# Turning the softmax weights of sixteen heads: 32 x 32 squares on VectorE and a way through DRAM in place of TensorE transposes

## The chip, the cores and the metric

The kernel runs on one core of a Trainium2 chip. The metric is the device time of one execution in microseconds (us). Before the change three runs took 2202.40, 2202.78 and 2203.02 us, a median of 2202.78 us. The engines are called by the profile's names: PE is TensorE's matmul, PEld its weight load, DVE is VectorE, ACT is ScalarE, POOL is GpSimd, SP is SyncE. A "q" behind a name (SPq, POOLq) is the queue on which that engine issues transfers.

## The reference, cut to what matters

The model is a trunk of two layers for 256 tokens of 2048 features: a gated linear attention layer, then a cross-decoder layer with 16 heads of 128 features, each followed by a gated feed-forward network with a short convolution. The change touches the second layer's attention alone. With a block of 256 and a sequence of 256 there is only the query's own block, so it is plain causal attention with a bias by distance:

```python
def attend(c):
    ...
    s_own = jnp.einsum('bhqd,bhkd->bhqk', q_c, k_own).astype(jnp.float32)
    s_own = s_own + bias_table[:, rel_bucket(dist_own)][None]
    s_own = jnp.where(dist_own >= 0, s_own, -jnp.inf)
    scores = jnp.concatenate([s_sel.reshape(B, H, QC, topk * BLK), s_own], axis=-1)
    p = jax.nn.softmax(scores, axis=-1).astype(v_blk.dtype)
    ...
    return (jnp.einsum('bhqjk,bhqjkd->bhqd', p_sel, v_sel)
            + jnp.einsum('bhqk,bhkd->bhqd', p_own, v_own))
```

Keys and queries are normed per head first. The weights p come out with queries on the rows; the product with v contracts over keys, so p is needed with keys on the rows, that is, turned.

## The kernel before, in words

**Weights.** All large matmuls read float32 weights, split into a high part (`whi`, a cast to the reduced float type that TensorE takes) and a low rest (`wlo`). `WeightStream` cuts every weight matrix into chunks of 128 x 2048 (1 MB, three `wraw` buffers, loaded on SP's queue at L112) and each chunk into halves of 1024 columns. `prefetch` makes `whi` of a half on ScalarE (L132) and `wlo` on VectorE (L133); there are four buffers of each. `step` takes the next half; all other work hangs on these steps: `after(n, job)` puts a job n steps ahead, and `step` runs the jobs that are due before it takes its half.

**The stage around the change.** `gemm_tok` (L348) works through 16 row tiles in eight steps: per step eight matmuls with `whi` (L357) and four with `wlo` (L360) into one accumulator. It runs four times for the queries, four times for the keys (weights `w_kk`) and four times for the values (`w_kv`); each run covers four heads.

- `head_norm` (L917) norms a key group. ScalarE squares and copies (L921, L922), VectorE reduces (L924, L925), GpSimd takes a power (`rr`, L927), VectorE multiplies (L929).
- `features` (L932), three and four steps later, turns the group on TensorE (`tr`, L937), ScalarE and VectorE copy and split it (L940 to L943).
- `softmax` (L949), five to eight steps after the key group, does the scores of one head on TensorE (L953 for the first 128 queries against 128 keys, L955 three times for the other 128 queries against all 256 keys), then on VectorE adds the bias and finds the extreme (L962), on ScalarE takes the exponential with its sum (L964), on VectorE the reciprocal (L966) and the scaling (L968). The result `s` is 128 queries x 384: columns 0 to 127 for the first half of the queries, 128 to 383 for the second.
- `turn` (L971), two steps after each head's softmax, makes three 128 x 128 transposes on TensorE into the PSUM tile `pT` (L975). The first 256 columns of `pT` are split into a high and a low part in `p0` (`split`: L382 on ScalarE, L383 on VectorE), the last 128 are copied to `p1` on ScalarE (L981).
- `values` (L983), one and two steps after each value group, multiplies them with v (`mix`, L429, tile `o`) and splits the result (`ox`).

**Other work in the stage.** `make_ahead` (L306) prepares sums of the second feed-forward's down weights: SP loads a 1 MB plane into one of two `ahead` buffers (L314), VectorE does four additions (L311, L312), POOL writes it to DRAM (`tsum`, L321). Later in the kernel `turn_h` (L796) turns the residual by a VectorE transpose in squares of 32 (L801) and eight transfers on SP's queue with runs of 128 B (`hscr`, L807).

**Memory.** Small PSUM tiles (`s`, `pT`, `tr`, `o` and others) share two banks. Most SBUF tiles of the stage take one of 32 slots of equal size. Temporary tiles such as `s` take one of six.

**Order.** Each engine works through its own list in order. The lists come from a planner that models the time of each instruction; `tc.issue_after(x)` keeps what is inside it behind instruction x on the same engine. `ws.low` is the latest `wlo`, `ws.load` the latest weight load. Every instruction waits for what it reads and for the buffer it writes; a transfer also waits for its turn on one of eight completion counters per kind of queue.

Of the kernel before, what the change touches and what calls it, by code (L numbers as in the profile page):

```python
# [8 lines left out]
F32 = mybir.dt.float32  # L9
# [16 lines left out]
MH = 16  # L26
# [32 lines left out]
class WeightStream:  # L59
# [58 lines left out]
    def prefetch(self, i):  # L118
        nc = self.nc
        while self.n_split < len(self.halves):  # L120
            n = self.n_split
            c, o, width, deep = self.halves[n]
            if n > i + self.AHEAD + deep:
                break
            self._dma(c + 1)
            t = self.tiles[c]
            src = t[o // 1024] if isinstance(t, list) else t[:, o:o + width]
            hi = self.parts.tile([128, 1024], F32R, name="whi")
            lo = self.parts.tile([128, 1024], F32R, name="wlo")
            for a, b in ((0, 512), (512, 1024)) if n < 2 else ((0, src.shape[1]),):  # L130
                with self.tc.issue_after(self.first) if n + a else nullcontext():
                    nc.scalar.copy(hi[:, a:b], src[:, a:b])  # L132
                self.low = nc.vector.tensor_sub(lo[:, a:b], src[:, a:b], hi[:, a:b].bitcast(F32))  # L133
            self.split[n] = (hi, lo)
            self.n_split += 1
            if self.chunks[c][-1] == n:
                del self.tiles[c]
                self._dma(c + (6 if c in self.quads else 4))
# [7 lines left out]
def trunk(ctx: ExitStack, tc: tile.TileContext, xT, cst, msk, w1p, w2a, w_k, w_qa, w_v2, w_v, w_g, w_go,  # L146
          w_up0, w_dn0, w_kk, w_kv, w_mq, w_mo, w_up1, w_dn1, rel, onehot, out):
    nc = tc.nc
    V, A, T = nc.vector, nc.scalar, nc.tensor
# [9 lines left out]
    dram = ctx.enter_context(tc.tile_pool(name="dram", bufs=1, space=DRAM))  # L159

    def slot(shape, dt, name):
        return big.tile(shape, dt, name=name, tag="slot")
# [4 lines left out]
    def bank(name, shape):  # L167
        return mis_ps.tile(list(shape), F32, name=name, tag="bank")

    ws = WeightStream(tc, raw, parts)  # L170
# [4 lines left out]
    for layer, todo in enumerate(ahead):  # L175
        t = dram.tile([len(todo), 128, 2048], F32, name=f"tsum{layer}")
# [55 lines left out]
    ident = mk[:, 0:128]  # L232
# [70 lines left out]
    def after(steps, job):  # L303
        later.append((cur[0] + steps, job))
# [43 lines left out]
    def gemm_tok(xs, groups=1):  # L348
        out_ = [acc_ps.tile([128, 2, 512], F32, name="acc") for _ in range(groups)]
        for q0 in range(0, KT, 2):  # L350
            for ps in out_:
                hi, lo = step()
                for ks in ((0,), (1,)) if cur[0] < 3 and groups > 1 else ((0, 1),):
                    tiles_ = [(q0 + k, t, k * 512) for k in ks for t in range(2)]
                    for x0 in (0, S):
                        for kt, t, c in tiles_:
                            T.matmul(ps[:, t, :], xs(kt)[:, x0 + 128 * t:x0 + 128 * t + 128], hi[:, c:c + 512],  # L357
                                     start=kt == 0 and x0 == 0, stop=False)
                    for kt, t, c in tiles_:
                        T.matmul(ps[:, t, :], xs(kt)[:, 128 * t:128 * t + 128], lo[:, c:c + 512],  # L360
                                 start=False, stop=kt == KT - 1)
        ws.prefetch(cur[0])
        return out_ if groups > 1 else out_[0]
# [4 lines left out]
    def both(ps, name):  # L368
        t = temp(name)
        A.copy(t, ps[:, :, S:])  # L370
        V.tensor_add(t, t, ps[:, :, :S])
        return t
# [8 lines left out]
    def split(dst_hi, dst_lo, src):  # L381
        A.copy(dst_hi, src)  # L382
        V.tensor_sub(dst_lo, src, dst_hi.bitcast(F32))  # L383
# [124 lines left out]
    for hd in range(GH):  # L508
        ps = gemm(xs, KT)
        rstd = nrm.rstd  # L510
        k = both(ps, "k")
        V.tensor_mul(k, k, bc(rstd))
        b = bcum[hd]
# [64 lines left out]
    for hd in range(GH):  # L578
        ps = gemm(xs, KT)
        q = both(ps, "q")  # L580
# [11 lines left out]
    for hd in range(GH):  # L592
        for c in range(2):
            ps = gemm(xs, KT)
            g = both(ps, "g")
# [321 lines left out]
    def head_norm(ps, name):  # L917
        t_, sq = slot([128, 2, 512], F32, name), slot([128, 2, 512], F32, "hsq")
        for t in range(2):
            r = n_q.col[:, t:t + 1]  # L920
            A.activation(sq[:, t, :], ps[:, t, :], AF.Square, scale=r)  # L921
            A.activation(t_[:, t, :], ps[:, t, :], AF.Copy, scale=r)  # L922
        ss = small.tile([128, 8], F32, name="ss")
        V.tensor_reduce(ss, sq.rearrange("p t (h d) -> p (t h) d", d=128), axis=AX.X, op=OP.add)  # L924
        V.tensor_scalar(ss, ss, 1.0 / 128, EPS, op0=OP.mult, op1=OP.add)  # L925
        rr = small.tile([128, 8], F32, name="rr")
        nc.gpsimd.tensor_tensor(rr, ss, mhalf, op=OP.pow)  # L927
        u = t_.rearrange("p t (h d) -> p (t h) d", d=128)
        V.tensor_mul(u, u, rr[:, :, None].to_broadcast([128, 8, 128]))  # L929
        return t_  # L930

    def features(t_, c, f, scale, c0):  # L932

        tp = bank("tr", (128, 2, S))
        for i in range(2):
            for t in range(2):
                T.transpose(tp[:, i, 128 * t:128 * t + 128],  # L937
                            t_[:, t, (2 * c + i) * 128:(2 * c + i + 1) * 128], ident)
        whole, halves_ = f[0][:, 2 * c:2 * c + 2, :], f[1][c]
        A.activation(whole, tp[:, :, :128], AF.Copy, scale=scale)  # L940
        hi, lo = halves_[:, :, 0, :], halves_[:, :, 1, :]
        A.activation(hi, tp[:, :, c0:], AF.Copy, scale=scale)
        V.scalar_tensor_tensor(lo, tp[:, :, c0:], scale, hi.bitcast(F32), op0=OP.mult, op1=OP.subtract)  # L943

    qf, kf, ox = [], [], []
    pts = [None] * MH
    p0s, p1s = [], []

    def softmax(hd):  # L949
        (q0, q1), (k0, k1) = qf[hd // 4], kf[hd // 4]  # L950
        q1, k1 = q1[hd // 2 % 2][:, hd % 2], k1[hd // 2 % 2][:, hd % 2]
        sp = bank("s", (128, 384))
        T.matmul(sp[:, 0:128], q0[:, hd % 4, :], k0[:, hd % 4, :], start=True, stop=True)  # L953
        for i, (a, b) in enumerate(((0, 0), (0, 1), (1, 0))):
            T.matmul(sp[:, 128:384], q1[:, a, :], k1[:, b, :], start=i == 0, stop=i == 2)  # L955
        s = temp("s", (128, 384))
        st = small.tile([128, 4], F32, name="st")
        bt = bias[hd // 4][:, hd % 4, :]
        for t, (c0, c1) in enumerate(((0, 128), (128, 384))):
            n = c1 - c0  # L960
            rev = bass.AP(tensor=bt.tensor, offset=bt.offset + n - 1, ap=[bt.ap[0], [-1, n]])
            V.tensor_tensor_reduce(s[:, c0:c1], sp[:, c0:c1], rev, -1.0, 3.0e38, OP.add, OP.min,  # L962
                                   st[:, t:t + 1])
            A.activation(s[:, c0:c1], s[:, c0:c1], AF.Exp, bias=st[:, t:t + 1], scale=-1.0,  # L964
                         accum_out=st[:, 2 + t:3 + t])
        V.reciprocal(st[:, 2:4], st[:, 2:4])  # L966
        for t, (c0, c1) in enumerate(((0, 128), (128, 384))):
            V.tensor_scalar(s[:, c0:c1], s[:, c0:c1], st[:, 2 + t:3 + t], None, op0=OP.mult)  # L968
        pts[hd] = s

    def turn(hd):  # L971
        s = pts[hd]
        tp = bank("pT", (128, 384))
        for c in range(3):
            T.transpose(tp[:, 128 * c:128 * c + 128], s[:, 128 * c:128 * c + 128], ident)  # L975
        if hd % 8 == 0:
            p1s.append(slot([128, 8, 128], F32, "p1"))
        if hd % 2 == 0:
            p0s.append(slot([128, 2, 2, S], F32R, "p0"))
        split(p0s[-1][:, hd % 2, 0], p0s[-1][:, hd % 2, 1], tp[:, :256])  # L980
        A.copy(p1s[-1][:, hd % 8], tp[:, 256:])  # L981

    def values(v, p):  # L983
        op = bank("o", (128, 2, S))
# [14 lines left out]
    for g in range(4):  # L999
# [5 lines left out]
        f = (q8[:, g % 2 * 4:g % 2 * 4 + 4], (q1[:, 0:2], q1[:, 2:4]))  # L1005
# [4 lines left out]
    for g in range(4):  # L1010
        ps = gemm_tok(xs)
        t_ = head_norm(ps, "k")
        if g % 2 == 0:
            k8 = slot([128, 8, 128], F32, "k0")
        f = (k8[:, g % 2 * 4:g % 2 * 4 + 4], [slot([128, 2, 2, S], F32R, f"k1{c}") for c in range(2)])
        kf.append(f)
        for c in range(2):
            after(3 + c, lambda t_=t_, c=c, f=f: features(t_, c, f, kqw, 0))
        for i in range(4):
            after(5 + i, lambda i=i, g=g: softmax(4 * g + i))  # L1020
            after(7 + i, lambda i=i, g=g: turn(4 * g + i))
    for g in range(4):
        ps = gemm_tok(xs)
        if g % 2 == 0:
            vm1 = slot([128, 2, 512], F32, "vm1")
        v = (slot([128, 2, 512], F32R, "vm0"), vm1[:, g % 2, :])
        v_out(v, ps, n_q)
        for c in range(2):
            after(1 + c, lambda v=v, p=2 * g + c: values(v, p))
# [115 lines left out]
```

## Time and profile before

| | |
|---|---|
| profiled execution | 2202.72 us, of which the span from the first to the last instruction is 2200.8 us |
| granted TensorE clock | 1.000 |
| transferred | 592.40 MB, mean 269 GB/s |
| transfers of 8 KB packets for weights on SP's queue (q1) | 514.79 MB, 66.1% of the 16 DMA engines |
| transfers on POOL's queue (q0) | 75.06 MB, 8.9% |
| packets under 512 B | 27,953 of 108,152 |
| transposes of the softmax weights (`pT`, L975) | 48, from 1241.4 to 1372.4 us |
| GpSimd busy over the span | 83.9 us |

How to read the profile's views: the page gives busy time by engine; matmuls overlap and their ends are modelled, so a busy TensorE is read from the chain of waits and not from its share. The chain lists the work that ended last, followed back from the end. A row of a timeline has the start, the duration, the engine, the line, the operation, the tiles (out <- in), and in brackets the idle time before it with what ended it. A row of the waits has: who waited, for whom, us in total, how often, the longest. Rows of transfers give the destination, the source, the queue, the count, the size of one and the median time from issue to landing.

### The profile page before, as it was taken

How to read it: one execution, taken by the hardware profiler on the slowest of the kernel's cores; microseconds unless marked ns; L12 is line 12 of the kernel's file. 1: busy time of each engine (PE TensorE's matmuls, PEld its weight loads, DVE VectorE, ACT ScalarE, POOL GpSimd, SP SyncE). 2: the span in 40 equal slices, each digit the busy share in tenths (PEclk: the TensorE clock that was granted, in tenths of full speed). 3: DMA queues.
4: the chain of work that ended last, by engine and by line, in shares of the span. 5: the costliest groups of instructions: out<-in, count | busy, mean ns of one | idle time of the engine just before them, and what ended most of it. 6: DMA issues, size and time to landing. Idle time of an engine off the chain costs nothing.

```text
span 2200.8 us, 31104 instructions
## 1 busy us (share of the span) xinstructions
PE 2194.0 (100%) x11689; PEld 1895.5 (86%) x11689; DVE 1763.6 (80%) x2547; ACT 1316.7 (60%) x1840; POOL 83.9 (4%) x134
## 2 busy tenths in 40 slices
PE   9999999999999999999999999999999999999999
PEld 7889888888888888888888888888888888888887
DVE  6676877888888887877777777678988888878887
ACT  6655654655566555666656655546655665556565
POOL 0000000000000000000001100000000000000000
PEclk9999999999999999999999999999999999999999
DMA  8675678777777776887768666677788777878895
GB/s 286 212 263 207 232 271 302 270 262 274 270 271 268 278 273 212 303 333 287 279 248 295 240 222 241 220 266 264 270 282 280 276 271 279 289 259 310 330 369 205
DMA packets 108152, 592.40 MB, mean 269 GB/s; under 512 B 27953, under 2 KB 28481, under 8 KB 45282
## 3 DMA queue, kind: packets, MB, share of 16 engines
q1 hardware_dynamic: 93170, 514.79, 66.1%
q0 software_dynamic: 14256, 75.06, 8.9%
q8 instruction: 91, 1.49, 0.3%
q10 hardware_dynamic: 576, 0.58, 0.1%
q14 instruction: 59, 0.48, 0.1%
HBM read 522.99 MB, written 67.40 MB: 268 GB/s over the span
## 4 chain that ended last, share of the span: by engine, by line
PE 99%; DMA 0%; ACT 0%; DVE 0%; SPq 0%; issue 0%
PE acc L342 40%; PE acc L344 21%; PE acc L736 14%; PE acc L357 10%; PE p L736 6%; PE acc L360 5%; PE sT L548 0%; DMA wraw<-w_v 0%; PE tr L937 0%; PE s L955 0%; PE pT L975 0%; PE z L454 0%; PE s L953 0%; PE o L434 0%; PE oT L434 0%; DMA gn<-cst 0%
## 5 line engine op out<-in xcount | busy, mean ns | idle before, releaser
L132 ACT CAST whi<-wraw 128x1024 fp32r<-128x1024 f32 (+1 forms) x786 | 799.1, 1020 | 629.1 <-PE acc L342 308.4
L133 DVE TENSOR_TENSOR wlo<-wraw,whi 128x1024 fp32r<-128x1024 f32 (+1 forms) x786 | 920.3, 1182 | 278.0 <-ACT whi L132 98.3
L342 PE MATMUL acc<-xw,whi 128*128 128x512 f32 x3328 | 795.5, 391 | 0.0
L342 PEld LDWEIGHTS acc<-xw,whi 128*128 128x128 f32 x3328 | 611.1, 188 | 117.9
L344 PEld LDWEIGHTS acc<-xw,wlo 128*128 128x128 f32 x3328 | 427.2, 191 | 16.2
L344 PE MATMUL acc<-xw,wlo 128*128 128x256 f32 x3328 | 433.4, 283 | 0.0
L736 PE MATMUL acc<-whi,hid 128*128 128x512 f32 x596 | 173.9, 390 | 0.0
L133 DVE TENSOR_TENSOR wlo<-ahead,whi 128x1024 fp32r<-128x1024 f32 x92 | 112.3, 1224 | 37.7 <-ACT whi L132 22.2
L357 PE MATMUL acc<-whi,xkv 128*128 128x512 f32 x512 | 132.7, 393 | 0.0
L357 PE MATMUL acc<-whi,xw 128*128 128x512 f32 x512 | 129.8, 393 | 1.5 <-ACT whi L132 1.5
L736 PEld LDWEIGHTS acc<-whi,hid 128*128 128x128 f32 x596 | 111.4, 188 | 22.8
L132 ACT CAST whi<-ahead 128x1024 fp32r<-128x1024 f32 x92 | 96.3, 1054 | 56.8 <-PE p L736 44.3
L736 PE MATMUL p<-whi,hid 128*128 128x512 f32 x386 | 124.7, 389 | 0.0
L357 PEld LDWEIGHTS acc<-whi,xw 128*128 128x128 f32 x512 | 95.3, 189 | 22.2 <-ACT whi L132 2.4
L357 PEld LDWEIGHTS acc<-whi,xkv 128*128 128x128 f32 x512 | 94.4, 188 | 18.3
L685 ACT ACTIVATE au<-up,cs 128x256 f32<-128x256 f32 x176 | 96.1, 593 | 7.6 <-DVE up L681 7.6
L687 DVE SCALAR_TENSOR_TENSOR au<-up,cs,au 128x255 f32<-128x255 f32 x176 | 82.9, 478 | 18.9 <-ACT au L685 18.8
L736 PE MATMUL acc<-wlo,hid 128*128 128x512 f32 x298 | 97.1, 389 | 0.0
L736 PE MATMUL acc<-whi,comb 128*128 128x512 f32 x320 | 95.6, 389 | 0.0
L736 PEld LDWEIGHTS p<-whi,hid 128*128 128x128 f32 x386 | 72.4, 188 | 15.1
L370 ACT COPY up<-acc 128x512 f32<-128x512 f32 x88 | 51.6, 586 | 47.0 <-PE acc L344 46.0
L689 DVE SCALAR_TENSOR_TENSOR au<-up,cs,au 128x254 f32<-128x254 f32 x176 | 79.5, 476 | 0.0
(264 smaller groups left out, 2184.7 us busy)
## 6 DMA issues: line engine op xcount, KB each, us to landing
wraw<-w_up SPq DMA_DIRECT2D x176, 1024.0 KB, 5.1
ahead<-w_dn SPq DMA_DIRECT2D x53, 1024.0 KB, 9.1
tsum<-ahead POOLq DMA_DIRECT2D x53, 1024.0 KB, 7.8
ahead<-tsum SPq DMA_DIRECT2D x46, 1024.0 KB, 6.0
wraw<-w_dn SPq DMA_DIRECT2D x53, 768.0 KB, 5.7
wraw<-w_dn SPq DMA_DIRECT2D x35, 1024.0 KB, 6.1
wraw<-w_g SPq DMA_DIRECT2D x16, 1024.0 KB, 5.7
wraw<-w_go SPq DMA_DIRECT2D x16, 1024.0 KB, 5.9
```

What stands on the lines that cost most here:

```text
L132: nc.scalar.copy(hi[:, a:b], src[:, a:b])
L133: self.low = nc.vector.tensor_sub(lo[:, a:b], src[:, a:b], hi[:, a:b].bitcast(F32))
L342: T.matmul(ps[:, b, :], two[i][0][:, c:c + 128], xs(kt), start=kt == 0, stop=False)
L344: T.matmul(ps[:, b, :S], two[i][1][:, c:c + 128], xs(kt)[:, :S], start=False, stop=kt == kts - 1)
L357: T.matmul(ps[:, t, :], xs(kt)[:, x0 + 128 * t:x0 + 128 * t + 128], hi[:, c:c + 512], start=kt == 0 and x0 == 0, stop=False)
L360: T.matmul(ps[:, t, :], xs(kt)[:, 128 * t:128 * t + 128], lo[:, c:c + 512], start=False, stop=kt == KT - 1)
L370: A.copy(t, ps[:, :, S:])
L685: A.activation(au[:, i, :], t[:, i, :], AF.Identity, bias=col(cb + n), scale=col(cw + 2 * 2 * FT + n))
L687: V.scalar_tensor_tensor(au[:, i, 1:], t[:, i, :S - 1], col(cw + 2 * FT + n), au[:, i, 1:], op0=OP.mult, op1=OP.add)
L689: V.scalar_tensor_tensor(au[:, i, 2:], t[:, i, :S - 2], col(cw + n), au[:, i, 2:], op0=OP.mult, op1=OP.add)
L736: T.matmul(p[n], x[xi], w[wi][:, 512 * f:512 * f + 512], start=n not in begun, stop=left[n] == 0)
```

## The change

`turn` no longer uses TensorE. It takes a slot tile `t` of two times 384 columns, lets VectorE transpose `s` in squares of 32 x 32 into the first half (L977 of the changed kernel), writes each quarter of 32 partitions to a DRAM tile `turned` with runs of 32 values (L980, four transfers on GpSimd's queue), and reads the head back with keys on the partitions into the second half (L981, one transfer on the same queue). The VectorE transpose is kept behind the latest `wlo`. The split into `p0` and the copy to `p1` move to a new job `weights`, eight steps after `turn`, kept behind the latest `whi` cast on ScalarE.

```diff
             for a, b in ((0, 512), (512, 1024)) if n < 2 else ((0, src.shape[1]),):
                 with self.tc.issue_after(self.first) if n + a else nullcontext():
-                    nc.scalar.copy(hi[:, a:b], src[:, a:b])
+                    self.high = nc.scalar.copy(hi[:, a:b], src[:, a:b])
                 self.low = nc.vector.tensor_sub(lo[:, a:b], src[:, a:b], hi[:, a:b].bitcast(F32))
...
+    turned = dram.tile([MH, 12, 32, 128], F32, name="turned")
+
     def turn(hd):
-        s = pts[hd]
-        tp = bank("pT", (128, 384))
-        for c in range(3):
-            T.transpose(tp[:, 128 * c:128 * c + 128], s[:, 128 * c:128 * c + 128], ident)
+
+        t = slot([128, 2, 384], F32, "pT")
+        with tc.issue_after(ws.low.ins):
+            V.transpose(t[:, 0], pts[hd])
+        to = turned[hd].rearrange("f b (m a) -> m b f a", a=32)
+        for m in range(4):
+            nc.gpsimd.dma_start(to[m], t[32 * m:32 * m + 32, 0].rearrange("b (f a) -> b f a", a=32))
+        nc.gpsimd.dma_start(t[:, 1].rearrange("k (j q) -> k j q", j=3),
+                            turned[hd].rearrange("(j f) b q -> (f b) j q", f=4))
+        pts[hd] = t[:, 1]
+
+    def weights(hd):
+        tp = pts[hd]
         if hd % 8 == 0:
             p1s.append(slot([128, 8, 128], F32, "p1"))
         if hd % 2 == 0:
             p0s.append(slot([128, 2, 2, S], F32R, "p0"))
-        split(p0s[-1][:, hd % 2, 0], p0s[-1][:, hd % 2, 1], tp[:, :256])
-        A.copy(p1s[-1][:, hd % 8], tp[:, 256:])
+        with tc.issue_after(ws.high.ins):
+            split(p0s[-1][:, hd % 2, 0], p0s[-1][:, hd % 2, 1], tp[:, :256])
+            A.copy(p1s[-1][:, hd % 8], tp[:, 256:])
...
             after(5 + i, lambda i=i, g=g: softmax(4 * g + i))
             after(7 + i, lambda i=i, g=g: turn(4 * g + i))
+            after(15 + i, lambda i=i, g=g: weights(4 * g + i))
```

## The prediction

> **What bounds the kernel now.** I read the page first: span, busy shares, and the chain of work that ended last.
>
> ```profile
> span 2200.8 us, 31104 instructions
> PE 2194.0 (100%) x11689; PEld 1895.5 (86%) x11689; DVE 1763.6 (80%) x2547; ACT 1316.7 (60%) x1840; POOL 83.9 (4%) x134
> ...
> PE 99%; DMA 0%; ACT 0%; DVE 0%; SPq 0%; issue 0%
> ```
>
> TensorE is never without work, and 99% of the chain is its own. But shares are averages, so the stage of the change comes next: the same chain in order of time, from 1200 to 1420 us.
>
> ```profile
> by line: PE acc L357 51.3%; PE acc L360 25.7%; PE acc L342 6.8%; PE acc L344 3.5%; PE s L955 2.6%; PE pT L975 2.4%; PE tr L937 2.0%; PE s L953 1.6%; PE o L434 1.6%; PE o L432 0.9%; PE o L433 0.9%; PE o L431 0.9%
> ...
> 1231.29 1.81 PE acc L357 x8
> 1233.10 0.91 PE acc L360 x4
> 1234.01 0.68 PE acc L357 x3
> 1234.91 0.35 PE s L955 x3
> 1235.48 0.36 PE s L955 x3
> ...
> 1255.90 0.33 PE pT L975 x3
> 1256.46 1.84 PE acc L357 x8
> ...
> 1303.10 0.88 PE tr L937 x8
> ```
>
> A weight half (a "step") is 8 L357 and 4 L360 matmuls, 1.81 + 0.91 = 2.72 us, 0.227 us each; a head's scores take 0.57 us (1234.91 to 1235.48). The three transposes of a head stand in the chain with 0.33 us. Does TensorE wait for the weight stream here, or the stream for TensorE? The waits from 1230 to 1400 us, one cast, and the busy times of the stage say:
>
> ```profile
> ACT whi L132 <- PE acc L357: 30.9, 23, 2.4
> ACT p L382 <- PE pT L975: 9.2, 8, 1.7
> ```
>
> ```profile
> 1233.14 1.05 ACT L132 CAST whi<-wraw 128x1024 fp32r<-128x1024 f32 x1 [1.66 <-PE acc L357]
> ```
>
> ```profile
> 1230.00:1380.00 150.00, 150.00 (x746) 125.91 (x745) 108.72 (x216) 90.64 (x176) 9.12 (x7) 1.00 0.67 239
> ```
>
> The columns of the last are PE, PEld, DVE, ACT and POOL busy, the clock, the DMA share and GB/s. The casts wait for TensorE to release a buffer: this one starts at 1233.14, as the L357 of its step end at 1233.10. There are four such buffers, so it fills the one needed four steps on: 0.91 + 3 x 2.72 - 1.05 = 8.0 us of cushion. ScalarE, and much the same VectorE, may stand still for 8 us before TensorE does. So the stage is TensorE's, and what leaves its order shortens the run.
>
> **What is removed.** 16 heads x 0.33 us = 5.28 us. The eight matmuls after the quoted transposes took 1.84 instead of 1.81 us, so each break costs 0 to 0.03 us, 0 to 0.5 in all; I take 0.4. In the order of the changed program the scores also stand in pairs, eight breaks less, 0 to 0.2 us; I take none. Gain 5.7 us, bounds 5.3 to 6.0. All else must be hidden; each part follows with its cover.
>
> **VectorE.** Sixteen stream transposes of 128x384. The nearest row is the one of 128x512:
>
> ```profile
> L801 DVE STREAM_TRANSPOSE hT<-h x8: 701/704/707, 1515.6 to 1705.5; 128x512 f32<-128x512 f32 x8
> ```
>
> By columns 0.53 us, at most 0.70: 8.5 to 11.3 us in all. I take 0.53 each. VectorE goes from 108.7 to about 117 us of 150; behind a transpose stands at most the next wlo, with its 8 us. Nothing on the path. The copies of the turned weights (p, L382, L383, L981) stay and read SBUF instead of PSUM; the cast of the same 128x256 from PSUM and one from SBUF:
>
> ```profile
> L382 ACT CAST p<-pT x16: 349/373/398, 1242.4 to 1372.8; 128x256 fp32r<-128x256 f32 x16
> ```
>
> ```profile
> 1515.97 0.39 ACT L382 CAST hid<-au 128x256 fp32r<-128x256 f32 x1
> ```
>
> 0.02 us each, 0.3 in all under the same cushion: nothing.
>
> Each head's turned tile also takes one of the 32 slots; in the changed order the waits that come of it are for transfers of heads two groups back: nothing.
>
> **GpSimd's queue.** 64 writes (32 partitions x 12 runs of 128 B, 384 runs, 48 KB) and 16 reads (128 x 3 runs of 512 B, again 384, 192 KB).
>
> ```profile
> 1156.22 2.30 POOL L913 DMA_DIRECT2D bias<-bscr  x3 [4.18 <-PE acc L357]
> 1163.84 0.76 POOL L913 DMA_DIRECT2D bias<-bscr  x1 [5.33 <-issue]
> ...
> 1248.55 2.69 POOL L927 TENSOR_TENSOR rr<-ss,mhalf 128x8 f32<-128x8 f32 x1 [21.68 <-DVE ss L925]
> 1256.46 0.57 POOL L321 DMA_DIRECT2D tsum<-ahead  x1 [5.22 <-DVE s L968]
> ```
>
> An issue takes 0.57 us (tsum, 128 runs) to 0.77 (bias, 512 runs of 1 KB); I take 0.7, 56 us in all on an engine busy for 9 of 150. The first two rows tell more: the fourth bias load began 5.3 us late, waiting for nothing the profile shows, 7.6 us after the first was issued, which is what such a load takes to land (below). I read it as room for descriptors: 3 x 512 runs fit, 4 x 512 do not. Of our 384 then four are in flight for certain and a fifth (1920 runs) perhaps; I take five. So POOL issues five DMAs per landing time.
>
> ```profile
> tsum<-ahead POOLq DMA_DIRECT2D x53, 1024.0 KB, 7.8
> hspill<-h POOLq DMA_DIRECT2D x8, 256.0 KB, 4.7
> bias<-bscr POOLq DMA_DIRECT2D x4, 512.0 KB, 7.6
> hscr<-hT SPq DMA_DIRECT2D x64, 32.0 KB, 4.6
> res<-hscr POOLq DMA_DIRECT2D x8, 256.0 KB, 6.0
> bscr<-brow POOLq DMA_DIRECT2D x1, 24.0 KB, 4.1
> ```
>
> A write lands in 4.1 to 7.8 us; I take the 4.6 of hscr, same runs of 128 B. A read: 4.7 to 7.8, I take 6.0 (res). Mean of four and one: 4.9 us. The Trainium skill, "DMA: Bandwidth & Descriptors", section "Anatomy of one DMA — SWDGE (gpsimd) path", fits 2.0 us plus bytes over 436 GB/s, an estimate of 2.1 us a write and 2.5 a read, by which rival (1) below would fall away. The trace disagrees: bscr takes 4.1 us for 24 KB.
>
> **Who waits behind them.** In the changed order a group of four heads lasts 110 weight matmuls x 0.227 + 4 x 0.57 + 0.88 = 28.1 us. Its 20 DMAs take 20/5 x 4.9 = 19.6 us and rr 2.7: 22.3, it fits. With four in flight it is 27.2 and just fits. rr, which VectorE needs for L929 before the features (tr) on TensorE, stands behind eight writes of two heads; VectorE has some 6 us of other work between L925 and L929, and tr comes about 5 us after that, so rr may be 8 us late. tsum stands behind writes too. Its buffer is one of two, so the load that SP issues next (1261.11) takes the other, and the tsum of 1256.46 has to land only by the one after, 36 us on; SP's queue, with the weights behind that load, is not held.
>
> ```profile
> 1261.11 0.45 SPq L314 DMA_DIRECT2D ahead<-w_dn  x1
> ...
> 1292.71 0.89 SPq L314 DMA_DIRECT2D ahead<-w_dn  x1
> ```
>
> The tightest place is the last group, where sixteen writes stand ahead of four reads. Count from the end of the last transpose; that of head 14 ended 2.2 us before. Head 14's fourth write lands at 4.5 and read 12 goes, landing at 10.5. ScalarE reaches that copy after two ox copies and four casts paced by 2.72 us, at about 8, and stands for 2.5 us. Head 14's first write lands at 4.6 - 2.2 = 2.4, which lets the second write of head 15 go; that lands at 7.0, read 14 goes and lands at 13.0, as ScalarE comes to it (about 13). The cast behind is too late from about 19. Margin 6 us: no stall, and elsewhere the eight steps (8 x 2.72 = 21.8 us) leave 3 us and more beside the cushion.
>
> **The DMA engines.** Two windows of 1 us, one full of runs of 128 B to DRAM, one of 8 KB loads:
>
> ```profile
> DMA packets 1093, 0.17 MB, mean 171 GB/s; under 512 B 1088, under 2 KB 1088, under 8 KB 1088
> ...
> q1 hardware_dynamic: 1093, 0.17, 94.7%
> ```
>
> ```profile
> DMA packets 53, 0.43 MB, mean 434 GB/s; under 512 B 0, under 2 KB 0, under 8 KB 0
> ...
> q1 hardware_dynamic: 53, 0.43, 102.7%
> ```
>
> 0.947 x 16 us / 1093 = 13.9 ns for 128 B; 0.31 us for 8 KB, which is 4.8 ns per 128 B. Writes: 24,576 x 13.9 / 16 = 21 us of all engines. Reads: 6,144 x 19 ns (by bytes) to 56 ns (four short packets) / 16 = 7 to 21 us. Together 28 to 43, I take 30, against 0.33 x 150 = 50 us free. The share goes to about 0.87. The weights are loaded three 1 MB buffers deep, two steps each, so a load may take some 10.9 us (4 x 2.72), twice what it takes now:
>
> ```profile
> wraw<-w_kv SPq DMA_DIRECT2D x16, 1024.0 KB, 5.2
> ```
>
> **Sum.** 2202.72 (this execution; 1.9 us outside its span stay) - 5.7 = 2197.0; the median of the runs is 0.06 higher, so 2197.1 us. Its own range is 2196.4 to 2198.3.
>
> **Rivals.** (1) Slower: the room for descriptors paces the stage. If these DMAs land like bias and tsum, in 7.6 us, because they share the engines with each other and the weights, a group needs 4 x 7.6 + 2.7 = 33.1 us where TensorE takes 28.1: 5 us lost per group, 15 over three intervals, and in the last group read 14 lands at 3 x 7.6 - 2.2 = 20.6, 1.6 too late. ScalarE stands at the copies, the casts run out, TensorE waits: 2197.1 + 16.6 = 2214 us. It decides from a mean landing of (28.1 - 2.7) / 4 = 6.4 us (5.1 with four in flight). For it: two of six rows are above that. Against: those move 512 KB and 1 MB; the small ones land in 4.1 to 4.7.
>
> (2) Only the last group, or one tr behind a late rr, stalls by 2 to 7 us and eats the gain: 2199 to 2204, middle 2201.
>
> (3) The DMA engines become the bound. From 50 us x 16 / 30,720 packets = 26 ns per packet the loads fall behind; at 40 ns the stage grows by 27 us: 2197 + 27 = 2224. Against: 13.9 ns. The Trainium skill, "VectorE: DVE Perf Modes", section "The three transpose paths", warns that a plain DMA copy which transposes by access-pattern strides is 19x slower than the crossbar. At 19 x 4.8 ns a packet that would be an estimate of about 2295 us. The trace shows 2.9x for these runs, since 32 values stay together.
>
> (4) TensorE is not the bound here and the gap is refilled by weight waits: 2202.8. Against: the 30.9 us that casts wait for TensorE.
>
> **Chances.** Forecast 0.56; (1) 0.22; (2) 0.14; (3) 0.04; (4) 0.04. A difference under 0.2% (4.4 us) I count as no change. Faster: the forecast, 0.56. Slower than 2207.2: (1) and (3), 0.26. Same: (2) and (4), 0.18. The range 2196.2 to 2211 holds the forecast, (2), (4) and the milder half of (1).
>
> **What would show it.** Right: pT gone from the chain, its rows still contiguous TensorE, copies p on ScalarE waiting for DMA no more than 2 to 3 us at a time, turned landing under 6 us, and L977 at about 0.53 us. Wrong: POOL rows with several us of "issue" ahead of the writes, long waits "ACT p" on a DMA, casts that no longer wait for TensorE, TensorE in the chain broken by DMA or ACT between 1250 and 1400 us. A DMA share near 1 there would point to (3).

## The result, and the profile after

The changed kernel takes 2197.02 us (median of 10 runs, 2196.66 to 2197.53), the kernel before 2202.8 (10 runs, 2202.4 to 2203.03). The ratio is 0.9974, with a 95% interval of 0.9966 to 0.9982: 5.8 us less. The prediction was 2197.1. From the page of the changed kernel, span, busy times and the chain by engine:

```profile
span 2195.4 us, 31162 instructions
...
PE 2188.0 (100%) x11641; PEld 1890.7 (86%) x11641; DVE 1770.9 (81%) x2563; ACT 1315.8 (60%) x1840; POOL 134.6 (6%) x214
...
PE 99%; DMA 1%; ACT 0%; DVE 0%; SPq 0%; issue 0%
```

TensorE is busy 6.0 us less (2194.0 before) in 48 matmul instructions fewer, and it is still nearly the whole chain. VectorE has 7 us more, GpSimd 51 us more, and none of it shows in the span. The chain of the stage, 1200 to 1420 us, and three of its rows in order of time:

```profile
by line: PE acc L357 51.3%; PE acc L360 25.6%; PE acc L342 8.5%; PE acc L344 4.3%; PE s L955 2.6%; PE tr L937 2.0%; PE o L434 1.6%; PE s L953 1.6%; PE o L432 0.9%; PE o L433 0.9%; PE o L431 0.9%
...
1254.83 0.91 PE acc L360 x4
1255.74 0.68 PE acc L357 x3
1256.42 0.87 PE tr L937 x8
```

`PE pT` (2.4% before) is gone, and no other line has taken its place: L342 and L344 are the next project, which begins earlier. The rows join without a gap. The waits from 1230 to 1400 us (engine, line, waited for what: us in all, times, the longest) and the busy times of the stage:

```profile
ACT whi L132 <- PE acc L357: 44.3, 35, 1.7
...
POOL turned L980 <- issue: 10.9, 10, 2.2
...
POOL pT L981 <- DMA turned<-pT: 3.9, 1, 3.9
...
ACT p L993 <- DMA pT<-turned: 2.2, 2, 1.8
...
ACT p L382 <- DMA pT<-turned: 1.7, 2, 1.2
```

```profile
1230.00:1380.00 150.00, 150.00 (x743) 126.94 (x742) 119.86 (x237) 93.80 (x183) 58.98 (x87) 1.00 0.82 282
```

The casts still wait for TensorE, 44.3 us where it was 30.9: the weight side has not lost its lead. The copies of the turned weights wait for a DMA four times, 1.8 us at the longest, and TensorE waits for nothing in this stretch. The DMA share is 0.82, before 0.67.

### The profile page after: what moved, and what is told of

The parts are those of the page before. It is cut to its first block, busy times and chain, and to the rows that moved or that the text cites. A ratio compares the mean times of both kernels' runs of the same rounds, so it can differ in the third digit from the quotient of the medians.

```text
span 2195.4 us, 31162 instructions
## 1 busy us (share of the span) xinstructions
PE 2188.0 (100%) x11641; PEld 1890.7 (86%) x11641; DVE 1770.9 (81%) x2563; ACT 1315.8 (60%) x1840; POOL 134.6 (6%) x214
## 4 chain that ended last, share of the span: by engine, by line
PE 99%; DMA 1%; ACT 0%; DVE 0%; SPq 0%; issue 0%
PE acc L342 40%; PE acc L344 21%; PE acc L736 14%; PE acc L357 10%; PE p L736 6%; PE acc L360 5%; PE sT L548 0%; DMA wraw<-w_v 0%; PE tr L937 0%; PE s L955 0%; DMA gn<-cst 0%; PE z L454 0%; PE o L434 0%; PE oT L434 0%; PE s L953 0%; PE oT L433 0%
## 5 line engine op out<-in xcount | busy, mean ns | idle before, releaser
L342 PE MATMUL acc<-xw,whi 128*128 128x512 f32 x3328 | 795.5, 391 | 0.0
L342 PEld LDWEIGHTS acc<-xw,whi 128*128 128x128 f32 x3328 | 611.1, 188 | 117.9
L344 PEld LDWEIGHTS acc<-xw,wlo 128*128 128x128 f32 x3328 | 427.2, 191 | 16.2
L344 PE MATMUL acc<-xw,wlo 128*128 128x256 f32 x3328 | 433.4, 283 | 0.0
L321 POOL DMA_DIRECT2D tsum<-ahead x53 | 28.8, 543 | 1085.7 <-DVE ahead L312 1008.8
```

What stands on the lines that cost most here:

```text
L321: after(8, lambda: nc.gpsimd.dma_start(parked[layer][at], t))
L342: T.matmul(ps[:, b, :], two[i][0][:, c:c + 128], xs(kt), start=kt == 0, stop=False)
L344: T.matmul(ps[:, b, :S], two[i][1][:, c:c + 128], xs(kt)[:, :S], start=False, stop=kt == kts - 1)
```

## Experiments

There are eleven. Except where said, each is an edit of the changed kernel. The kernel before ran beside them at 2202.7 to 2202.9 us.

### 1 and 2: is it TensorE's time alone?

Experiment 1 takes the kernel before and leaves the transposes out:

```diff
         s = pts[hd]
-        tp = bank("pT", (128, 384))
-        for c in range(3):
-            T.transpose(tp[:, 128 * c:128 * c + 128], s[:, 128 * c:128 * c + 128], ident)
+        tp = s
```

> The kernel before, with the 48 TensorE transposes of the weights left out and nothing in their place: the weights that go into values are the unturned ones, so that part of the computation is missing. No stream transposes, no transfers, copies at the place they had before. If the whole effect of the change is TensorE's 16 x 0.33 us and the breaks around them, this gives the time of the changed kernel, 2197.0 (ratio 0.997 to the kernel before, 2196.5 to 2197.6), and the round trip by way of DRAM costs nothing. If the changed kernel also pays something for the round trip (late copies, one stall at the last group) this comes out below it by that price, 2196 or less. If the gain came from the later split and not from TensorE, this stays near 2202.

Experiment 2 puts them back into the changed kernel:

```diff
     def turn(hd):
+        tp = bank("pT", (128, 384))
+        for c in range(3):
+            T.transpose(tp[:, 128 * c:128 * c + 128], pts[hd][:, 128 * c:128 * c + 128], ident)
         t = slot([128, 2, 384], F32, "pT")
```

> The changed kernel, with the 48 TensorE transposes put back beside the stream transposes, into a bank that nobody reads. TensorE as the bound: the 5.3 to 6.0 us come back, 2202.3 to 2203.0, ratio to the kernel before 1.000 (0.9995 to 1.0005). Rival, that the gain is the freed bank, the later split or the new order of the copies: it keeps the gain, 2197 to 2198.5.

| kernel | us | runs from to | ratio to before, interval |
|---|---|---|---|
| before | 2202.8 | 2202.4 to 2203.0 | 1 |
| changed | 2197.02 | 2196.7 to 2197.5 | 0.9974 (0.9966 to 0.9982) |
| 1, no transposes, nothing instead | 2196.71 | 2196.4 to 2197.7 | 0.9973 (0.9963 to 0.9984) |
| 2, both transposes | 2202.74 | 2202.5 to 2203.6 | 1.0001 (0.9992 to 1.001) |

Experiment 2 loses the whole gain, 5.72 us, with the round trip still in it; its chain of the stage has the line back (the edit shifts it to L977), at the old 2.4%:

```profile
by line: PE acc L357 51.2%; PE acc L360 25.7%; PE acc L342 6.9%; PE acc L344 3.5%; PE s L955 2.6%; PE pT L977 2.4%; PE tr L937 2.0%; PE o L434 1.6%; PE s L953 1.6%; PE o L433 0.9%; PE o L432 0.9%; PE o L431 0.9%
```

So neither the later split nor the order of the copies brought anything that these runs can show. Experiment 1, which has no round trip at all, is 0.31 us below the changed kernel, less than the spread of either: the round trip is hidden, but for some 0.3 us.

### 3, 4 and 9: the room for descriptors

The prediction read from a late bias load that GpSimd's queue has room for only so many transfers, took five in flight, and had that room as its first rival. The size of the room is a number of the program:

```diff
-    nc = bacc.Bacc("TRN2", target_bir_lowering=False, num_devices=1, dynamic_dma_scratch_size=2048)
+    nc = bacc.Bacc("TRN2", target_bir_lowering=False, num_devices=1, dynamic_dma_scratch_size=1536)
```

It is 1792 in experiment 4 and 2560 in experiment 9.

> The changed kernel with the room for descriptors of GpSimd's queue cut from 2048 to 1536 bytes: where five turned transfers were in flight at once, three should be. Theory (the queue has room to spare and becomes the pace below some number): a group of four heads issues 20 transfers, 20 / 3 x 4.7 us + 1.7 us for rr = 33 us, against the 28.1 us that a group of the stage lasts; the turned weights come later by 5 us a group. Eight steps are 17 us, less the round trip of about 15 us; so two or three groups late, the cast waits and TensorE with it: slower than the changed kernel by 10 to 25 us, 2207 to 2222. Rival, that the transfers are not held by that room (the 1.8 us before the sixth is something else): 2197, no change.

> The same with 1792 bytes, four in flight: 20 / 4 x 4.7 + 1.7 = 25 us, still under the 28.1 us of a group: 2197 to 2199. If a landing takes longer when fewer descriptors are queued, or rr comes late, up to 2204.

> The changed kernel with 2560 bytes of room for descriptors, so that six turned transfers fit where five did. Below five each step cost time (2203.6 with four, 2222.3 with three). If the fifth was already enough: 2197, no change, and above it lie only the 0.3 us to the kernel without any turn (2196.7). If the room still paces a part of the stage: 2196.7 or less.

GpSimd's first turned writes, in the changed kernel, with 1536 and with 2560 bytes (start, us, line, how many one after the other, idle before and what ended it):

```profile
1238.83 3.10 POOL L980 DMA_DIRECT2D turned<-pT  x5 [11.63 <-DVE st L966]
1243.71 1.87 POOL L980 DMA_DIRECT2D turned<-pT  x3 [1.77 <-issue]
```

```profile
1238.90 1.90 POOL L980 DMA_DIRECT2D turned<-pT  x3 [11.62 <-DVE st L966]
1244.29 1.98 POOL L980 DMA_DIRECT2D turned<-pT  x3 [3.49 <-issue]
```

```profile
1238.29 3.71 POOL L980 DMA_DIRECT2D turned<-pT  x6 [11.46 <-DVE st L966]
1243.46 1.22 POOL L980 DMA_DIRECT2D turned<-pT  x2 [1.47 <-issue]
```

Five, three, six (and four with 1792 bytes): the "issue" ahead of the next is the wait for room. In the changed kernel the first write lands 4.6 us after its issue at 1238.83, and the sixth goes 0.3 us later (1243.71). A count of 384 runs each doesn't give these numbers (4 x 384 = 1536, but 1536 bytes held three). The trace shows 16 packets of 4 bytes with every transfer; with them it is 400 each, which fits all four settings and the late bias load of the prediction (4 x 528 = 2112). That count is a reading of these rows and was not tested by itself. What each number costs:

| room, bytes | in flight | us | runs from to |
|---|---|---|---|
| 1536 | 3 | 2222.29 | 2221.6 to 2222.8 |
| 1792 | 4 | 2203.61 | 2198.1 to 2206.7 |
| 2048 (the change) | 5 | 2197.02 | 2196.7 to 2197.5 |
| 2560 | 6 | 2196.76 | 2196.3 to 2197.1 |

The sixth in flight brings 0.26 us, less than the spread. Three give 2222.3 us, just above the 2207 to 2222 that were expected (whose eight steps are 21.8 us, not 17). This is the rival "the room paces the stage", seen from the other side: the room is real, and the change stands one step away from its price. With three in flight, the waits of ScalarE and of TensorE, one of the stalls, and the windows of the stage (PE, PEld, DVE, ACT, POOL busy; clock; DMA share; GB/s; then two windows of 10 us) say where the time goes:

```profile
ACT p L382 <- DMA pT<-turned: 35.6, 7, 10.6
```

```profile
PE s L953 <- DVE st L962: 12.6, 2, 7.4
PE tr L937 <- DVE k L929: 2.6, 1, 2.6
```

```profile
1344.34 0.40 ACT L382 CAST p<-pT 128x256 fp32r<-128x256 f32 x1 [7.67 <-DMA pT<-turned]
...
1344.77 0.42 DVE L383 TENSOR_TENSOR p<-pT,p 128x256 fp32r<-128x256 f32 x1 [7.30 <-ACT p L382]
...
1345.81 0.79 PE L953 MATMUL s<-k,q 128*128 128x128 f32 x2 [5.17 <-DVE st L962]
```

```profile
1260.00:1290.00 30.00, 27.36 (x135) 22.85 (x134) 21.07 (x49) 18.05 (x40) 13.50 (x20) 1.00 0.69 231
1290.00:1320.00 30.00, 22.60 (x100) 18.84 (x99) 19.17 (x49) 14.95 (x36) 9.04 (x15) 0.83 0.70 248
1320.00:1350.00 30.00, 24.83 (x115) 20.82 (x114) 18.50 (x35) 13.42 (x27) 13.26 (x20) 0.89 0.79 258
1350.00:1380.00 30.00, 28.34 (x133) 23.52 (x132) 19.71 (x38) 15.25 (x32) 11.58 (x18) 0.96 0.68 223
```

```profile
1300.00:1310.00 10.00, 2.60 (x13) 2.32 (x12) 2.75 (x11) 3.52 (x12) 2.18 (x4) 0.63 0.84 306
1320.00:1330.00 10.00, 10.00 (x50) 8.37 (x49) 9.01 (x12) 5.34 (x8) 5.88 (x8) 1.00 0.76 231
```

ScalarE stands at the copies, up to 10.6 us, and TensorE is idle for 16.9 us in the four long windows (120 less 103.13). None of its waits is for a cast of weights. Most are at the scores (L953): VectorE's half of the copy (L383) waits for ScalarE's, behind it in VectorE's order stands the bias step (L962) of the heads before, and the next scores wait for that. This way has less lead than the 8.0 us of the casts: in the stall shown ScalarE stood 7.67 us, and TensorE lost 5.17.

The rest is the clock. TensorE is busy 2195.4 us in the profiled execution and 2188.0 in that of the changed kernel, with the same 11641 matmuls: 7.4 us more. 16.9 + 7.4 = 24.3, which is what the span is longer (2219.7 to 2195.4). In windows of 2 us the granted clock is 0.50 from 1304 to 1312, after TensorE stopped at 1300.3 and went on at 1307.7, and 1.00 again from 1314; the two later stalls bring such a fall each. So the idle time comes in four pieces, 2.6 (`tr` behind a late `rr`), 7.4, 5.2 and 1.6 us, as the theory of a late group had it (33 us a group expected); but nearly a third of the loss is the clock, which it did not have.

With four in flight the sum said 25 us a group, under TensorE's 28.1, so 2197 to 2199. Most of the 11 runs are above that. In its profiled run (2200.8 us) the median landings are not longer than in the changed kernel, but the longest are (writes, then reads; min, median, max), and GpSimd's waits are:

```profile
DMA to landing us min/median/max: 2.0/4.2/9.2
```

```profile
DMA to landing us min/median/max: 2.9/4.4/12.0
```

```profile
POOL turned L980 <- issue: 31.5, 12, 6.6
...
POOL turned L980 <- DVE pT L977: 10.2, 3, 4.9
```

In the changed kernel the longest write took 6.3 us, the longest read 9.9. The queue stands 31.5 us at a full room, and besides it waits in order for VectorE's transposes, which a sum of mean landings leaves out. So the decision point of the prediction, a mean landing of 5.1 us with four in flight, was too kind: the queue needs slack, here one transfer more. ScalarE waits for a copy up to 3.8 us in the middle of this stage, and TensorE loses 0.7 us there in all; at the last heads it waits 7.2 us, and TensorE loses 1.6 at the product with the values.

### 5 and 6: the eight steps

```diff
-            after(15 + i, lambda i=i, g=g: weights(4 * g + i))
+            after(11 + i, lambda i=i, g=g: weights(4 * g + i))
```

and 9 + i in experiment 6.

> The changed kernel with the weights made four steps (10.9 us) after the turn instead of eight (21.8 us). In the trace of the changed kernel the turned weights of a head are back 15 to 20 us after its stream transpose begins. If the eight steps hide a round trip that really lasts that long: the copies wait 5 to 9 us for the first head of a group and some more for the next ones, of which ScalarE and VectorE can catch up 8 us; 2199 to 2215. Rival, that the round trip is short or the place of the copies does not matter: 2197, no change.

> The same with two steps (5.4 us), where the copies stood in the kernel before. First theory: 5.4 us more of waiting for each of the four groups than with four steps, about 20 us above that run: 2215 to 2235. Rival: 2197.

Four steps: 2197.0 us (2196.1 to 2197.2, 7 runs), no change. The rival of the expectation came true, but it says little on the round trip: in the trace the first stream transpose starts at 1237.89 and its cast at 1257.33, 19.4 us later, where eight steps gave 20.9 us (1237.83 and 1258.77) and four steps fewer should have taken 10.9 off. The planner has placed most of the copies as far from their transposes as with eight steps. What a true lag of four steps costs wasn't tried.

Two steps: 2218.89 us (2216.4 to 2220.4, 4 runs; ratio 1.0074, 1.0058 to 1.0089). Here the copies do come early. The second stream transpose starts at 1240.11 and its cast, which had to wait for the DMA, at 1254.82: 14.7 us is the round trip of this head, with the first head's writes, 2.2 us of waiting for room and 2.5 us of `rr` on GpSimd in it. The worst place is later, on ScalarE and on TensorE:

```profile
1363.02 1.05 ACT L132 CAST whi<-wraw 128x1024 fp32r<-128x1024 f32 x1 [1.67 <-PE acc L357]
1367.39 0.41 ACT L382 CAST p<-pT 128x256 fp32r<-128x256 f32 x1 [3.32 <-DMA pT<-turned]
1367.70 0.29 ACT L993 COPY p<-pT 128x128 f32<-128x128 f32 x1
1367.90 1.26 ACT L942 ACTIVATE k<-tr,kqw 128x512 fp32r<-128x512 f32 x2
```

```profile
PE s L953 <- DVE k L943: 5.5, 1, 5.5
```

The wait itself is 3.3 us, but behind the cast in ScalarE's order stand the key features (L942), behind these VectorE's part (L943), and behind that the scores, for which TensorE waits 5.5 us. Without the 3.3 us some 2.2 us of that would be left (an estimate, 5.5 less 3.3), since the features themselves stand behind the copies in this order. So the price of a late copy is set by what stands behind it too. The expected size was met (2215 to 2235), its working was not: not 5 us in each group, since TensorE doesn't stand at all before 1320 us, but the features and scores of the later heads, and a mean clock of 0.84 from 1350 to 1380 us.

### 7: the same transfers on SyncE's queue

```diff
-            nc.gpsimd.dma_start(to[m], t[32 * m:32 * m + 32, 0].rearrange("b (f a) -> b f a", a=32))
-        nc.gpsimd.dma_start(t[:, 1].rearrange("k (j q) -> k j q", j=3),
+            nc.sync.dma_start(to[m], t[32 * m:32 * m + 32, 0].rearrange("b (f a) -> b f a", a=32))
+        nc.sync.dma_start(t[:, 1].rearrange("k (j q) -> k j q", j=3),
```

> The changed kernel with the 80 turned transfers on SyncE's queue instead of GpSimd's. No room of GpSimd's is used, but each transfer stands in order between the weight loads of 1024 KB, and behind the wait for its stream transpose stand the loads that are due next. If the loads are early enough (a ring of three raw buffers, 2.72 us a buffer): 2197 to 2199. If a waiting transfer holds up the loads by more than the cushion: 2200 to 2215. The transfers themselves, in this order, should take longer to be issued in the middle of the loads, so that the copies wait at some heads.

2200.16 us (2196.9 to 2205.8, 10 runs; ratio 0.9989, 0.998 to 0.9999): some of the gain, unsteadily. (A weight buffer of 1 MB feeds two steps, 5.4 us, and not the 2.72 us of the expectation.) In the profiled run (2201.2 us) TensorE is idle for 3.3 of the 150 us from 1230 to 1380. Loads and copies now wait:

```profile
ACT p L382 <- DMA pT<-turned: 8.1, 2, 7.6
ACT whi L132 <- DMA wraw<-w_kv: 7.8, 3, 3.8
```

More telling are the packets of the queues (q1 is the weights', q0 GpSimd's) from 1230 to 1380 us, in the changed kernel and then here:

```profile
DMA packets 8022, 42.31 MB, mean 282 GB/s; under 512 B 1840, under 2 KB 1840, under 8 KB 3632
...
q1 hardware_dynamic: 4217, 30.62, 58.4%
q0 software_dynamic: 3792, 11.54, 23.0%
```

```profile
q1 hardware_dynamic: 36171, 36.67, 77.7%
q0 software_dynamic: 720, 5.24, 8.4%
```

On SyncE's queue the 80 transfers add 36,171 - 4217 = 31,954 packets: one for each of their 80 x 384 = 30,720 runs, and nearly all the rest packets of 4 bytes. They add 77.7 - 58.4 = 19.3% of 150 us, 29 us of all engines. On GpSimd's they add 3792 - 720 = 3072 packets and 14.6%, 22 us, for the same 6 MB. Of these 3072 packets 1280 are the small ones, 16 for each transfer (1840 under 512 B, 560 in the kernel before). The other 1792 (3632 - 1840) carry the data; by their sizes in the trace 1024 hold 3 KB, 24 runs of 128 B, and 768 hold 4 KB, 8 runs of 512 B. So GpSimd's queue gathers runs into packets, and SyncE's does not. Whether the unsteady time comes from the larger share or from the transfers' place among the loads was not separated.

### 8, 10 and 11: the queries in the same way

TensorE also turns the query heads (32 of the `tr` transposes), and nobody needs them before the scores. Core of the edit of experiment 8:

```diff
+    def turn_q(t_, g):
+        t = slot([128, 1024], F32, "qT")
+        with tc.issue_after(ws.low.ins):
+            for i in range(2):
+                V.transpose(t[:, 512 * i:512 * i + 512], t_[:, i, :])
...
+        for i in range(2):
+            for m in range(4):
+                nc.gpsimd.dma_start(to[m, :, 16 * i:16 * i + 16],
+                                    t[32 * m:32 * m + 32, 512 * i:512 * i + 512].rearrange("b (f a) -> b f a", a=32))
...
+        after(2, lambda t_=t_, g=g: turn_q(t_, g))
         for c in range(2):
-            after(3 + c, lambda t_=t_, c=c, f=f: features(t_, c, f, 1.0, 128))
+            after(14 + c, lambda t_=t_, c=c, f=f: features(t_, c, f, 1.0, 128))
```

Experiment 10 is this with 2560 bytes of room, experiment 11 that with 20 + c for 14 + c.

> The changed kernel, with the 32 TensorE transposes of the query heads replaced in the same way: two stream transposes of 128x512, eight writes and four reads a group on GpSimd's queue, features eleven steps later. In the trace of the changed kernel these transposes cost 32 x 0.11 us = 3.5 us of TensorE, and nobody needs the queries before the keys are there. TensorE as the bound and the round trip hidden: 2193.5 (2193 to 2194.5). If the writes of 64 KB (twice the descriptors of those of the weights, so that three are in flight) last too long for a group of 28 us, or the queries of the last group come late for the first scores: 2196 to 2210.

> The kernel with the queries turned too, with 2560 bytes of room: four of its 64 KB writes in flight instead of three. It ran between 2194.4 and 2201.3. If its slow runs come from the room: all runs at 2193.5 to 2195. If they come from the transfers' order or the DMA engines (share 0.92 to 0.95 in two stretches): the spread stays, median 2197 to 2200.

> The same, with 2560 bytes, and with the query features seventeen steps after their place in the kernel before instead of eleven. If the casts of the query features wait for landings in its slow runs: 2193.5 to 2195 in all runs, the best of all kernels. If the stage is short of something else: no better than the run beside it.

| kernel | us | runs from to | ratio to before, interval |
|---|---|---|---|
| 8 | 2199.15 | 2194.4 to 2201.3 (11) | 0.9978 (0.997 to 0.9987) |
| 10, more room | 2193.61 | 2193.2 to 2195.8 (5) | 0.9961 (0.9948 to 0.9973) |
| 11, and features later | 2193.86 | 2193.3 to 2194.6 (5) | 0.996 (0.9946 to 0.9974) |

Experiment 8 comes near the expected 2193.5 in five of 11 executions (2194.4 to 2196.1), and in the others takes 2199 to 2201 us. Its 64 KB writes have 512 runs each, a third more than those of the weights (not twice, as the expectation has it), and its trace shows three of them in flight. With 512 bytes more no execution is above 2195.8. Experiment 10 has the lowest median: 9.1 us below the kernel before, 3.4 below the change, against 32 x 0.11 = 3.5 us of TensorE. That the room made the difference rests on 5 runs against 11; the profiled run of experiment 8 took 2195.0, so the place where its longer executions lose time was not seen.

The profiled run of experiment 10 is the longest of its five (2195.8), and it shows one such place between 1100 and 1260 us:

```profile
ACT q L961 <- DMA q<-turned_q: 3.1, 1, 3.1
```

```profile
PE acc L357 <- ACT xkv L242: 1.7, 1, 1.7
```

A copy of the query features waits 3.1 us for its transfer, behind it on ScalarE stands the operand of the key matmuls (`xkv`, L242), and TensorE waits 1.7 us for that. The profiled run of experiment 8 has the same pair, with 0.5 us for TensorE. In experiment 11, with later features, neither wait is left and TensorE waits for nothing there: the place was the one that its expectation named. The medians of 10 and 11 don't differ by more than their spread.

## Why the prediction was right

**The bound, and the gain.** Right, mechanism and size. The sum said 5.7 us (5.3 to 6.0); the medians differ by 5.8, putting the transposes back costs 5.72, taking them out without a replacement gives 6.0. The parts beside the 5.28 us (breaks 0.4, scores in pairs nothing) are smaller than what these runs can separate.

**The cushion.** The 8.0 us were worked out for the casts of weights alone, and the prediction let ScalarE and VectorE stand that long. That is not so for the copies: in experiment 3 ScalarE stood 7.67 us, VectorE 7.30, and TensorE lost 5.17, at the scores and not at a cast. The change was safe because its own waits stay at 1.8 us, not because of the 8.0.

**VectorE, ScalarE, GpSimd.** The rows of the new operations (ns min/median/max):

```profile
L980 POOL DMA_DIRECT2D turned<-pT x64: 615/618/700, 1238.8 to 1341.8; - x64
L977 DVE STREAM_TRANSPOSE pT<-s x16: 535/573/580, 1237.8 to 1335.5; 128x384 f32<-128x384 f32 x16
L981 POOL DMA_DIRECT2D pT<-turned x16: 748/753/768, 1249.7 to 1346.3; - x16
L382 ACT CAST p<-pT x16: 395/406/427, 1258.8 to 1352.7; 128x256 fp32r<-128x256 f32 x16
```

A stream transpose takes 0.573 us where 0.53 was taken by columns (bound 0.70), which is 9.2 us in all and not 8.5. VectorE has 120 us of 150 where 117 was expected; the rest is other work that moved into this window (experiment 1, with no stream transpose, has 111.9 us there, the kernel before 108.7). The cast from SBUF takes 0.406 us against 0.373 from PSUM: 0.03, predicted 0.02. An issue takes 0.62 or 0.75 us, predicted 0.7. None of it reached TensorE.

**The room for descriptors.** Five in flight, out of one late bias load: right to the unit (experiments 3, 4 and 9). That four would "just fit" was not: 2203.6 us.

**Landings.** Writes, then reads, in the changed kernel:

```profile
DMA to landing us min/median/max: 2.0/4.5/6.3
```

```profile
DMA to landing us min/median/max: 3.7/5.4/9.9
```

4.6 and 6.0 were taken, from hscr and res. The fit that the Trainium skill gives ("DMA: Bandwidth & Descriptors", section "Anatomy of one DMA — SWDGE (gpsimd) path"), by which a write would be 2.1 and a read 2.5 us, is met by the shortest writes alone. By that figure three in flight would need an estimate of 20 / 3 x 2.2 + 1.7 = 16 us a group, far under 28.1; experiment 3 disagrees.

**A group and the last group.** `tr` to `tr` is 28.2 us twice and then 29.8 (1228.24, 1256.42, 1284.61, 1314.38), predicted 28.1; the third has seven weight matmuls more in it, 117 and not 110. `rr` was early enough each time, since TensorE has no wait at all from 1230 to 1400 us. The last group, GpSimd:

```profile
1336.24 3.05 POOL L980 DMA_DIRECT2D turned<-pT  x5 [1.11 <-issue]
1341.21 1.23 POOL L980 DMA_DIRECT2D turned<-pT  x2 [1.92 <-issue]
1342.44 2.24 POOL L981 DMA_DIRECT2D pT<-turned  x3
1346.32 0.75 POOL L981 DMA_DIRECT2D pT<-turned  x1 [1.64 <-PE acc L357]
```

The last transpose ends at 1336.04. The first of the reads was to go 4.5 us later and went at 6.4; ScalarE was to stand 2.5 us at head 12's copy and stood 1.2. No stall, as said.

**The DMA engines.** A term outside its bounds: 28 to 43 us of all engines were expected, 30 taken; it was 22. The step that failed is "24,576 x 13.9 / 16": the 13.9 ns per run of 128 B had been read on SyncE's queue, and there experiment 7 finds 29 us. On GpSimd's queue the runs go in packets of 3 and 4 KB. The weights landed in 6.7 us where it had been 5.2, under the 10.9 that they may take. The warning of a 19 times slower transpose by strides ("VectorE: DVE Perf Modes", section "The three transpose paths" of the Trainium skill) did not come true for runs of 128 B on either queue: 29 and 22 us of all engines, where 6 MB at 4.8 ns per 128 B would be 15. No run here uses the crossbar.

**The rivals.** (1), the room, would have been the result with three in flight: 2222 us, against 2214 worked out for slow landings. The way to TensorE was another than (1) has it: there the casts did not run out, the scores came late. (2), a stall of a few us, is nearest to four in flight (2203.6); two steps cost more (2218.9), since TensorE stands at several places. (3) and (4) have no support: DMA share 0.82, and experiment 1 moved the time by TensorE's own share.

## What to carry to other kernels

Here work taken from the engine that is the chain came back one for one, because the detour stayed inside the lead of the engines that feed it; check that with two kernels, one without the work and one with both. Work out that lead for every way from the waiting instruction to the bound engine: the shortest counts, here the scores and not the weights. A detour over a DMA queue has a capacity of its own: count what is in flight, and give it more than the mean landing time asks for, because it is the long landings and the waits in the queue's order that stall. The price of a late result is set by what stands behind the waiting instruction, and not by the wait alone.

## What was not expected of the hardware

- GpSimd's queue moved runs of 128 B in packets of 3 KB and runs of 512 B in packets of 4 KB; on SyncE's queue each run was a packet of its own. 3072 packets against 31,954 for the same 80 transfers, 22 against 29 us of all engines.
- Room decides sharply: from five to four to three transfers in flight the time goes 2197.0, 2203.6, 2222.3 us, and at four one and the same program ran anywhere from 2198 to 2207.
- TensorE's granted clock fell to 0.50 after TensorE had stood some us, and was 1.00 again within 7 us of its going on (1307.7 to 1314 us in experiment 3). Over the whole run this cost 7.4 of the 24.3 us that experiment 3 lost.
